# Forget bias of the sample's keys: from two f32r pieces in operands of eight key places to three bf16 pieces in operands of four

## The chip, the core and the metric

The kernel runs on one core of a Trainium2 chip. Five engines work side by side, each through its own list of instructions in order: TensorE (PE in the profile, and PEld for its weight loads), VectorE (DVE), ScalarE (ACT), GpSimd (POOL) and SyncE (SP), which here does little but issue DMAs. The metric is the device time of one execution in microseconds; a kernel's time is the median of its runs.

## The reference

One inference step of a decoder layer for a prompt of 512 tokens and for a sample of 8 sequences with 8 new tokens each, whose past of 2048 keys lies in pages. Two attentions run side by side (forgetting attention, "fox", and a sparse attention, "nsa", of which the sample needs selected blocks, a window and compressed keys), then gates, projections and an MLP. The part that matters here is the forgetting attention of the sample:

```python
cf = jnp.cumsum(lf_all, axis=1)                       # running sum of the log forget values, per head
s = jnp.einsum('btgrd,bsgd->bgrts', q, k) * HEAD_DIM ** -0.5
bias = cq[..., :, None] - ck[..., None, :]            # sum of log forget values between key and query
p = masked_softmax(s + bias, k_pos <= q_pos)
```

Every key of the past gets, for each of 8 heads, the sum of the log forget values of all keys behind it, added to its scores. The sums must be good to about f32.

## The kernel before

The program runs in stages: compression of the sample's cached keys, the input projection, the prompt's attention (`prompt_attention`, at its end the "fox" steps), the sample's attention (`sample_attention`), then the gates and branch projections (`mix_part`, tiles `mg` and `br`), the output projection and the MLP. A scheduler orders the instructions of each engine by simulated times, so an added or shortened instruction can move its neighbours. In the sample's attention the order of PE is the order of the code: `link` ties each matmul behind the one before.

The sample's attention goes over 32 units, unit `u` being a quarter `i = u % 4` of the past of sequence `b = u // 4`, 512 keys each. On PE a round of its loop holds, in this order:

- `key_rows(u + 1)`: eight 128x128 transposes of the next unit's keys (tile `k`, from rows `fr` of the fox cache and `sr` of the nsa cache), copied to SBUF (`kt`) by ACT and by DVE.
- `unit_scores(u)`, L1691: the scores of both attentions in one PSUM bank `ss`. Partitions 0 to 63 hold fox (8 heads x 8 tokens), 64 to 127 nsa. Query times keys is an f32 matmul for each half (`bdF`, `bdN`, two passes each). Then comes the mask of selected blocks, one bf16 matmul of 512 columns into partitions 64 to 127 (L1699, `scr` in the profile), and then the forget bias, four matmuls of 128 columns into partitions 0 to 63 (L1702, `ss<-DT,E`).
- In the third unit of a sequence `new_scores` (tile `sn`) and, with it, `forget_turned(b + 1)` (tile `dt`); in every eighth unit (`u % 8 == 3`) `window_scores` (tile `sw`).
- `values(u - 3)` (tile `so`): weights times values as matmuls of 32 output partitions, and `turn_weights(u - 2)` (tile `sp`): four transposes of softmax weights, copied to `spT` by ACT and DVE in turn.

DVE takes the scores out of `ss` (`sS`, L1707) with the running maximum, ACT does the exponentials.

The forget bias is prepared in four steps. `Dt[p, b, c, h]` holds the log forget value of key place `c` (16 of them) on partition `p`. `forget_sums` (L682, near the end of the prompt's attention) adds up each half of 8 places, sums over the later partitions with one matmul (`xsuf`), and puts into place 0 and place 8 what lies behind their half. `forget_split` (L1674) splits 64 numbers (8 places x 8 heads) into an f32r part by ACT and a remainder by DVE, 2 x 64 rows for each half. `forget_turned` (L1681) turns both halves over with two PE transposes, and DVE copies them to `DT`. In `unit_scores` the constant `E` (zeros and ones from `tok` and `hot`) then adds, for key place `c`, the places behind it in its half and place 0 of the half. `DH` and `DT` have two buffers each, so the split for a sequence waits for the transposes of the second before it.

Loads of `fr` and `sr` are issued by SP about 7 units ahead, as buffers come free; the first units' loads follow right behind the prompt's attention.

Of the kernel before, what the change touches and what calls it, by code (L numbers as in the profile page):

```python
# [6 lines left out]
F32 = mybir.dt.float32  # L7
F32R = mybir.dt.float32r
BF16 = mybir.dt.bfloat16
I32 = mybir.dt.int32  # L10
AF = mybir.ActivationFunctionType
OP = mybir.AluOpType
AX = mybir.AxisListType

P = 128
# [3 lines left out]
NB = 8  # L19
# [26 lines left out]
class Step:  # L46
# [635 lines left out]
    def forget_sums(self, pn):  # L682


        self.scr, self.cut = pn.tile([P, 1024], F32, tag="wide", name="fscr"), 0
        triS = self.carve([P, P])
        self.ts(triS, self.jp, 0.0, None, OP.is_lt)
        half = self.carve([P, 2 * NB, 8])
        with self.tc.issue_after(self.last_min):
            self.nc.vector.tensor_reduce(half, self.Dt.rearrange("p b (a c) h -> p (b a) h c", a=2), axis=AX.X, op=OP.add)  # L690
        hv = half.rearrange("p (b a) h -> p b a h", a=2)
        tot = self.carve([P, NB, 8])
        self.tt(tot, hv[:, :, 0], hv[:, :, 1], OP.add)
        xb = self.accb("xsuf")
        self.mm(xb[:, 0:64], triS, tot.rearrange("p b h -> p (b h)"), True, True)
        xv = xb[:, 0:64].rearrange("p (b h) -> p b h", h=8)
        self.cp(self.Dt[:, :, 8, :], xv)
        self.tt(self.Dt[:, :, 0, :], xv, hv[:, :, 1], OP.add)

    def norm_scaled(self, sq, n, i, x, junk=None):  # L700

# [774 lines left out]
    def sample_tables(self):  # L1476


        nc, slope, gp = self.nc, self.slope, self.nc.gpsimd
        self.scr, self.cut = self.znp.tile([P, 4 * (TOK - C_N)], F32, tag="zN", name="scr"), 0  # L1480
        self.selT = self.carve([P, 256]).bitcast(BF16).rearrange("p (b n) -> p b n", b=NB)
        gp.memset(self.selT, 0.0)
        self.act(self.selT[:32], self.selF.rearrange("p (b n) -> p b n", b=NB))

        self.bhot = self.carve([P, 1024]).bitcast(BF16).rearrange("p (c n) -> p c n", c=16)

        self.nbA, self.nbW = self.carve([P, NB * 72]), self.carve([P, 320])
        self.rw = self.carve([P, SEQ])
        self.ramp = self.carve([P, 2048])
        mark = self.cut  # L1490
        self.cut -= 2048
        ei, hot = self.carve([P, 32]), self.carve([P, 32])
        self.iota(ei, [[1, 32]])
        self.ts(hot, ei, self.prow, None, OP.is_equal)
        self.act(self.bhot.rearrange("p c (a n) -> p (c a) n", a=2), hot[:, :, None].to_broadcast([P, 32, 64]))

        gp.memset(self.nbA, NEG)
        gp.memset(self.nbW, NEG)
        tmask, tramp = self.carve([P, NB, 8]), self.carve([P, NB, 8])
        self.iota(tmask, [[0, 8], [1, 8]])  # L1500
        self.ts(tramp, tmask, slope, None, OP.mult)
        self.ts(tmask, tmask, self.t_row, NEG, OP.is_gt, OP.mult)
        self.tt(tramp, tramp, tmask, OP.add)
        nbf = self.carve([NS, NB, 8])
        self.tt(nbf, self.nbf, tmask[:NS], OP.add)
        own = self.nbA.rearrange("p (b x) -> p b x", x=72)[:, :, 0:8]
        self.cp(own[0:64], nbf)
        self.cp(own[64:128], tramp[64:128])
        own = self.nbW.rearrange("p (i x) -> p i x", x=80)
        for o in range(2):  # L1510
            self.cp(own[64 * o:64 * o + 64, :, 8 * o:8 * o + 8], tramp[64 * o:64 * o + 64, 0:4])
        rw = self.rw
        self.iota(rw, [[1, 4], [4, P]])
        wm = self.carve([P, SEQ])
        self.ts(wm, rw, self.t_row, NEG, OP.is_le, OP.mult)
        self.ts(rw, rw, -512.0, slope, OP.add, OP.mult)
        self.tt(rw, rw, wm, OP.add)
        self.cut = mark


        self.tok, self.hot = self.carve([P, 8]), self.carve([P, 64])
        lim, ej = self.carve([P, 1]), self.carve([P, 8])
        self.iota(ej, [[1, 8]])
        self.ts(lim, self.h_row, 0.0, 8.0, OP.is_equal, OP.mult)
        self.tt(lim, lim, self.h_row, OP.add)
        self.ts(self.tok, ej, lim, None, OP.is_lt)
        self.ts(self.hot.rearrange("p (h t) -> p h t", t=8), ej[:, :, None].to_broadcast([P, 8, 8]), self.t_row, None, OP.is_equal)

        low = self.carve([P, 1])
        self.ts(low, self.prow, 64.0, slope, OP.is_ge, OP.mult)  # L1530
        self.iota(self.ramp, [[1, 2048]], base=-2048)
        gp.tensor_scalar(self.ramp, self.ramp, low, None, op0=OP.mult)
# [27 lines left out]

    def sample_attention(self, sp, sp0):
        nc = self.nc
        self.E = self.op2.tile([P, 8, 64], F32R, name="E")
        self.tt(self.E, self.tok[:, :, None].to_broadcast([P, 8, 64]), self.hot[:, None, :].to_broadcast([P, 8, 64]), OP.mult)
        self.chain = ""
        self.wk, self.S, self.SN, self.SW, self.DT, self.T, self.stat, self.OA = {}, {}, {}, {}, {}, {}, {}, {}
        self.sob, self.acc = self.accb("so"), self.accb("accS")
# [10 lines left out]
        for u in range(4 * NB + 4):  # L1578
            b, i, n, x = u // 4, u % 4, u // 8, u % 8
# [92 lines left out]
        self.keys[u] = out  # L1672

    def forget_split(self, sp, b):  # L1674
        self.DH = DH = self.op2.tile([P, 2, 2, 64], F32R, tag="DH", bufs=2, name=f"DH{b}")
        for hf in range(2):
            d = self.Dt[:, b, 8 * hf:8 * hf + 8, :].rearrange("p c h -> p (c h)")
            self.act(DH[:, hf, 0, :], d)
            self.tt(DH[:, hf, 1, :], d, DH[:, hf, 0, :].bitcast(F32), OP.subtract)

    def forget_turned(self, sp, b):  # L1681
        tb = self.mmb(f"dt{b}")
        for hf in range(2):
            self.tr(tb[:, P * hf:P * hf + P], self.DH[:, hf].rearrange("p a n -> p (a n)").bitcast(F32))
        self.DT[b] = self.op2.tile([P, 2, P], F32R, tag="DT", bufs=2, name=f"DT{b}")
        self.cp(self.DT[b], tb[:, 0:256].rearrange("p (a n) -> p a n", a=2))

    def queries(self, b):
        return [t[:, b].rearrange("p g r t -> p (g r t)") for t in (self.bdF, self.bdN)]
# [1 line left out]
    def unit_scores(self, sp, u):  # L1691

        b, i = u // 4, u % 4
        qF, qN = self.queries(b)
        kf, ks = self.keys.pop(u)
        pb = self.mmb(f"ss{u}")
        self.mm(pb[0:64, :], qF, kf, True, False)
        self.mm(pb[64:128, :], qN, ks, True, False)
        self.mm(pb[64:128, :], self.selT[:, b, :], self.bhot[:, 4 * i:4 * i + 4].rearrange("p c n -> p (c n)"), False, True)  # L1699
        for j in range(4):  # L1700
            c = 4 * i + j
            self.mm(pb[0:64, P * j:P * j + P], self.E[:, c % 8, :], self.DT[b][:, c // 8, :], False, True)  # L1702
        if i == 0:
            self.stat[b] = [self.small.tile(sh, F32, tag=f"ss{x}", name=f"ss{x}_{b}")
                            for x, sh in enumerate(([P, 2, 3], [P, 2, 3], [P, 2]))]
        self.S[u] = sp.tile([P, 512], F32, tag="S", bufs=4, name=f"sS{u}")
        self.nc.vector.tensor_tensor_reduce(self.S[u], pb, self.ramp[:, 512 * i:512 * i + 512], 1.0, LOW, OP.add, OP.max,  # L1707
                                            self.stat[b][0][:, i // 2, i % 2:i % 2 + 1])
# [724 lines left out]
```

## Time and profile before

| what | us |
|---|---|
| runs | 1212.0, 1212.29, 1216.9 |
| median | 1212.29 |
| profiled execution | 1216.62 |
| its span (first to last instruction) | 1214.9 |

The profiled execution is 4.3 us above the median, close to the slowest of the three. Sums are made against the profiled execution, and the difference is then taken from the median.

How the profile is read: a row of the timeline is start, duration, engine, line, operation, output <- inputs, shapes, count. Matmuls are pipelined, so the duration of one includes its way through the array (a 64-column bf16 weight load alone shows 0.11 us); what a matmul costs is the distance from its start to the start of the next. A row with x4 spans from the first start to the last end. All PE matmuls share line L77 and all transposes L83, so one goes by tiles.

| stretch of the span, us | what | PE busy | PE clock granted | DMA share |
|---|---|---|---|---|
| 395 to 437 | prompt's fox attention | 39.09 of 42 | 0.92 | 0.49 |
| 437 to 456 | its end, first keys of the sample | 17.41 of 19 | 1.00 | 0.31 |
| 592 to 700 | gates and branches | 107.21 of 108 | 1.00 | 0.54 |

The sample's attention lies between the last two rows.

### The profile page before, as it was taken

The numbers are of one execution on the slowest core, as the hardware profiler recorded it, in microseconds if no ns is written. First come the engines' busy times: TensorE is split into PE (matmuls) and PEld (weight loads), VectorE is DVE, ScalarE is ACT, GpSimd is POOL, SyncE is SP. The second block draws the span as 40 slices with busy tenths as digits, with TensorE's granted clock in tenths as the row PEclk, the third lists the DMA queues.
The fourth block names the chain that finished last, engine by engine and source line by source line (L and its number), as shares of the span: only waits on it lengthen the run. The fifth ranks groups of instructions, "written<-read, shape, count | busy, mean of one in ns | idle before, by whom it ended". The sixth has DMA issues, their size and how long they took to land.

```text
span 1214.9 us, 24824 instructions
## 1 busy us (share of the span) xinstructions
PE 1168.3 (96%) x9319; PEld 1003.8 (83%) x9319; DVE 768.3 (63%) x1984; ACT 557.8 (46%) x1187; POOL 155.0 (13%) x172
## 2 busy tenths in 40 slices
PE   3899999999999999999999999998999999999998
PEld 3887789899666556666799999998999997888886
DVE  3688785586798856665643335667667853655486
ACT  2455453443776754544532233355565655322230
POOL 1012100000311130000300100001455500000000
PEclk9999999999999999999999999998999999999999
DMA  9599546795776359979863334345344545446302
GB/s 209 161 246 272 167 149 216 239 321 176 240 259 180 90 169 301 316 230 297 204 175 87 87 83 134 108 142 184 129 146 138 173 149 188 150 162 200 109 28 79
DMA packets 168826, 215.37 MB, mean 177 GB/s; under 512 B 18297, under 2 KB 140610, under 8 KB 166530
## 3 DMA queue, kind: packets, MB, share of 16 engines
q1 hardware_dynamic: 147650, 174.21, 46.7%
q0 software_dynamic: 9216, 25.16, 6.7%
q10 hardware_dynamic: 11840, 14.42, 4.0%
q8 instruction: 73, 1.20, 0.4%
q14 instruction: 47, 0.39, 0.1%
HBM read 190.11 MB, written 44.53 MB: 193 GB/s over the span
## 4 chain that ended last, share of the span: by engine, by line
PE 82%; DMA 5%; DVE 5%; SPq 3%; ACT 2%; issue 1%; ACTq 0%; DVEq 0%; POOLq 0%
PE dn L77 16%; PE mg L77 8%; PE z L77 6%; PE hid L77 5%; PE ss L77 4%; PE br L77 4%; PE wo L77 4%; PE k L83 2%; SPq L155 2%; PE up L77 2%; PE so L77 2%; PE ct L83 2%; DMA cpg<-in_cache_nsa_kv 2%; PE sp L83 1%; PE ada L77 1%
## 5 line engine op out<-in xcount | busy, mean ns | idle before, releaser
L77 PE MATMUL z<-winh,h 128*128 128x264 f32 (+1 forms) x576 | 111.0, 286 | 1.1 <-ACT winh L112 0.8
L77 PEld LDWEIGHTS z<-winh,h 128*128 128x128 f32 x576 | 91.7, 190 | 3.2 <-ACT winh L112 1.0
L77 PE MATMUL z<-winl,h 128*128 128x264 f32 (+1 forms) x320 | 88.2, 284 | 0.5 <-DVE winl L131 0.5
L77 PE MATMUL mg<-hH,wml 128*128 128x288 f32 x256 | 75.3, 296 | 0.6 <-DVE wml L131 0.6
L112 ACT ACTIVATE xh<-ct 128x256 fp32r<-128x256 f32 x128 | 48.0, 384 | 59.9 <-PE ct L83 35.2
L77 PE MATMUL mg<-hH,wmh 128*128 128x288 f32 x256 | 75.3, 296 | 0.0
L100 DVE TENSOR_TENSOR acc<-acc,dn 128x512 f32<-128x512 f32 x60 | 41.2, 686 | 51.2 <-PE dn L77 51.1
L77 PE MATMUL mg<-hL,wmh 128*128 128x288 f32 x256 | 72.6, 294 | 0.0
L131 DVE TENSOR_TENSOR xl<-ct,xh 128x256 fp32r<-128x256 f32 x128 | 51.8, 421 | 15.7 <-ACT xh L112 13.9
L77 PEld LDWEIGHTS z<-winl,h 128*128 128x128 f32 x320 | 60.6, 190 | 0.7 <-DVE winl L131 0.7
L83 PE MATMUL ct<-identF,ro 128*128 128x128 f32 x256 | 36.0, 279 | 22.4 <-DVE ro L115 22.1
L131 DVE TENSOR_TENSOR wml<-wmr,wmh 128x1024 fp32r<-128x1024 f32 x14 | 17.2, 1226 | 56.4 <-ACT wmh L112 56.4
L83 PEld LDWEIGHTS ct<-identF,ro 128*128 128x128 f32 x256 | 29.5, 145 | 25.6 <-DVE ro L115 18.8
L77 PEld LDWEIGHTS mg<-hH,wml 128*128 128x128 f32 x256 | 48.1, 188 | 0.8 <-DVE wml L131 0.8
L77 PEld LDWEIGHTS mg<-hH,wmh 128*128 128x128 f32 x256 | 48.1, 188 | 0.2
L77 PEld LDWEIGHTS mg<-hL,wmh 128*128 128x128 f32 x256 | 47.2, 188 | 0.1
L131 DVE TENSOR_TENSOR wp<-sums,wp 128x1024 fp32r<-128x1024 f32 x26 | 39.9, 1541 | 11.0 <-ACT wp L112 10.3
L77 PE MATMUL hid<-xh,w1hlk 128*128 128x512 f32 (+1 forms) x160 | 44.9, 369 | 0.1
L77 PE MATMUL hid<-xh,w1hlv 128*128 128x512 f32 (+1 forms) x160 | 44.0, 361 | 0.8 <-ACT xh L112 0.5
L112 ACT ACTIVATE mgt<-mg 128x288 f32<-128x288 f32 x32 | 12.9, 410 | 59.6 <-PE mg L77 59.6
L1707 DVE CUSTOM_DVE_ANT_0 sS<-ss,scr 128x512 f32<-128x512 f32 x32 | 22.1, 692 | 26.2 <-PE ss L77 26.2
L112 ACT ACTIVATE u<-u 128x1152 f32<-128x1152 f32 x29 | 33.7, 1161 | 10.1 <-DVE u L100 9.4
(1160 smaller groups left out, 3643.4 us busy)
## 6 DMA issues: line engine op xcount, KB each, us to landing
adw<-in_w_ada SPq DMA_DIRECT2D x16, 1024.0 KB
foxD<-in_cache_fox_kv SPq DMA_DIRECT2D x128, 128.0 KB
wdr<-in_w_down SPq DMA_DIRECT2D x32, 512.0 KB
cpg<-in_cache_nsa_kv SPq DMA_DIRECT2D x120, 128.0 KB
fr<-foxD SPq DMA_DIRECT2D x28, 512.0 KB
sr<-in_cache_nsa_kv SPq DMA_DIRECT2D x112, 128.0 KB
pu<-in_w_up SPq DMA_DIRECT2D x26, 512.0 KB
uD<-u ACTq DMA_DIRECT2D x16, 576.0 KB
```

The costliest lines, as they stand in the source:

```text
L77: ins = self.nc.tensor.matmul(out, a, b, start=start, stop=stop, skip_group_check=True)
L83: ins = self.nc.tensor.transpose(out, in_, self.identF[:n, :n])
L100: self.nc.vector.tensor_tensor(out, a, b, op=op)
L112: return self.nc.scalar.activation(out, in_, f, **kw)
L131: self.splits.append((eng or self.nc.vector).tensor_tensor(l, x, h.bitcast(F32), op=OP.subtract).ins)
L155: self.issued[eng] = getattr(self.nc, eng).dma_start(out, in_).ins
L1707: self.nc.vector.tensor_tensor_reduce(self.S[u], pb, self.ramp[:, 512 * i:512 * i + 512], 1.0, LOW, OP.add, OP.max, self.stat[b][0][:, i / ...
```

## The change

The 16 places are cut into four quarters of 4 places instead of two halves of 8, and the numbers into three bf16 pieces that add up to the f32 number, instead of an f32r part and a remainder: 3 pieces x 4 places x 8 heads = 96 rows for an operand. `E` shrinks from 8 to 4 sets of 64 columns and becomes bf16. `forget_sums` writes places 0, 4, 8 and 12.

```diff
@@ forget_sums
-        half = self.carve([P, 2 * NB, 8])
+        part = self.carve([P, 4 * NB, 8])
         with self.tc.issue_after(self.last_min):
-            self.nc.vector.tensor_reduce(half, self.Dt.rearrange("p b (a c) h -> p (b a) h c", a=2), axis=AX.X, op=OP.add)
-        hv = half.rearrange("p (b a) h -> p b a h", a=2)
+            self.nc.vector.tensor_reduce(part, self.Dt.rearrange("p b (a c) h -> p (b a) h c", a=4), axis=AX.X, op=OP.add)
+        pv = part.rearrange("p (b a) h -> p b a h", a=4)
+        self.tt(pv[:, :, 2], pv[:, :, 2], pv[:, :, 3], OP.add)
+        self.tt(pv[:, :, 1], pv[:, :, 1], pv[:, :, 2], OP.add)
         tot = self.carve([P, NB, 8])
-        self.tt(tot, hv[:, :, 0], hv[:, :, 1], OP.add)
+        self.tt(tot, pv[:, :, 0], pv[:, :, 1], OP.add)
...
-        self.cp(self.Dt[:, :, 8, :], xv)
-        self.tt(self.Dt[:, :, 0, :], xv, hv[:, :, 1], OP.add)
+        self.cp(self.Dt[:, :, 12, :], xv)
+        for a in range(3):
+            self.tt(self.Dt[:, :, 4 * a, :], xv, pv[:, :, a + 1], OP.add)
@@ sample_tables
-        self.ts(lim, self.h_row, 0.0, 8.0, OP.is_equal, OP.mult)
-        self.tt(lim, lim, self.h_row, OP.add)
+        self.ts(pos, self.h_row, 4.0, -4.0, OP.is_ge, OP.mult)
+        self.tt(pos, pos, self.h_row, OP.add)
+        self.ts(lim, pos, 0.0, 4.0, OP.is_equal, OP.mult)
+        self.tt(lim, lim, pos, OP.add)
@@ sample_attention
-        self.E = self.op2.tile([P, 8, 64], F32R, name="E")
-        self.tt(self.E, self.tok[:, :, None].to_broadcast([P, 8, 64]), self.hot[:, None, :].to_broadcast([P, 8, 64]), OP.mult)
+        self.E = self.op2.tile([P, 4, 64], BF16, name="E")
+        self.tt(self.E, self.tok[:, 0:4, None].to_broadcast([P, 4, 64]), self.hot[:, None, :].to_broadcast([P, 4, 64]), OP.mult)
@@ forget_split
-        self.DH = DH = self.op2.tile([P, 2, 2, 64], F32R, tag="DH", bufs=2, name=f"DH{b}")
-        for hf in range(2):
-            d = self.Dt[:, b, 8 * hf:8 * hf + 8, :].rearrange("p c h -> p (c h)")
-            self.act(DH[:, hf, 0, :], d)
-            self.tt(DH[:, hf, 1, :], d, DH[:, hf, 0, :].bitcast(F32), OP.subtract)
+        self.DH = DH = self.op2.tile([P, 4, 3, 32], BF16, tag="DH", bufs=2, name=f"DH{b}")
+        rest = self.op2.tile([P, 4, 32], F32, tag="DR", bufs=1, name=f"DR{b}")
+        d = self.Dt[:, b].rearrange("p (a c) h -> p a (c h)", a=4)
+        self.act(DH[:, :, 0], d)
+        self.tt(rest, d, DH[:, :, 0], OP.subtract)
+        self.act(DH[:, :, 1], rest)
+        self.tt(DH[:, :, 2], rest, DH[:, :, 1], OP.subtract)
@@ forget_turned
-        for hf in range(2):
-            self.tr(tb[:, P * hf:P * hf + P], self.DH[:, hf].rearrange("p a n -> p (a n)").bitcast(F32))
-        self.DT[b] = self.op2.tile([P, 2, P], F32R, tag="DT", bufs=2, name=f"DT{b}")
-        self.cp(self.DT[b], tb[:, 0:256].rearrange("p (a n) -> p a n", a=2))
+        for a in range(4):
+            self.mm(tb[:96, P * a:P * a + P], self.DH[:, a].rearrange("p x n -> p (x n)"), self.identB, True, True)
+        self.DT[b] = self.op2.tile([P, 4, P], BF16, tag="DT", bufs=2, name=f"DT{b}")
+        self.cp(self.DT[b][:96], tb[:96].rearrange("p (a n) -> p a n", a=4))
@@ unit_scores
         for j in range(4):
-            c = 4 * i + j
-            self.mm(pb[0:64, P * j:P * j + P], self.E[:, c % 8, :], self.DT[b][:, c // 8, :], False, True)
+            self.mm(pb[0:64, P * j:P * j + P], self.E[:96, j, :], self.DT[b][:96, i, :], False, True)
```

The scheduler's answer moves instructions at three places that matter. The first is PE in a unit's scores, here the third unit of the first sequence, before (`scr` is the mask of selected blocks; an f32 or f32r matmul loads its weights itself and shows no row for it):

```order
L77 MATMUL ss_6703<-kt_2_6654,bdF 64x512
L77 MATMUL ss_6703<-kt_2_6661,bdN 64x512
L77 LDWEIGHTS scr
L77 MATMUL ss_6703<-scr 64x512
L77 MATMUL ss_6703<-DT_6460,E 64x128 x4
L77 MATMUL sn_6713<-knT,bdF 64x64
L77 MATMUL sn_6713<-knT,bdN 64x64
L83 MATMUL dt_6718<-identF,DH_6677 128x128 x2
```

And the same place now, up to the second of the four bias matmuls:

```order
L77 MATMUL ss_6713<-kt_2_6663,bdF 64x512
L77 MATMUL ss_6713<-kt_2_6670,bdN 64x512
L77 LDWEIGHTS scr
L77 MATMUL ss_6713<-scr 64x512
L77 LDWEIGHTS E
L77 MATMUL ss_6713<-DT_6469,E 64x128
```

The order is the same; each of the four bias matmuls now has a weight load of its own in front, and mask and bias are both bf16 and both 64 output partitions wide.

The second place, right behind it on PE, is the turning over of the next sequence's pieces (`dt`), now, from the fourth bias matmul to the first of four turning matmuls:

```order
L77 LDWEIGHTS E
L77 MATMUL ss_6713<-DT_6469,E 64x128
L77 MATMUL sn_6723<-knT,bdF 64x64
L77 MATMUL sn_6723<-knT,bdN 64x64
L77 LDWEIGHTS DH_6686
L77 MATMUL dt_6728<-identB,DH_6686 96x128
```

Two transposes of 128x128 have become four bf16 matmuls with the identity, 96 output partitions each.

The third place is DVE near the end of the prompt's attention, where it works through score tiles (`Sfox`), query tiles (`qstfox`) and tables of the sample side by side. Before:

```order
L109 SCALAR_TENSOR_TENSOR qstfox_5908<-qfox_5903,gcol,qstfox_5908 64x512
L100 TENSOR_TENSOR E<-scr 128x512
L309 TENSOR_REDUCE adw<-adat_6038 128x18
L1228 ISA Sfox_6140,nmfox_6141<-sfox_6144,browfox_5914 128x128
L1228 ISA nmfox_6141 128x1
```

And now:

```order
L109 SCALAR_TENSOR_TENSOR qstfox_5908<-qfox_5903,gcol,qstfox_5908 64x512
L100 TENSOR_TENSOR scr<-scr 128x1
L309 TENSOR_REDUCE adw<-adat_6038 128x18
L1231 ISA Sfox_6142,nmfox_6143<-sfox_6146,browfox_5914 128x128
L1231 ISA nmfox_6143 128x1
```

The making of `E` has left this place; with half the columns it stands 18 rows further down, and a 1-column instruction for `lim` stands here instead. On PE two score tiles of this stretch (256 and 384 columns) now stand ahead of eight `ofox` matmuls instead of behind them. SP's list is unchanged row by row, and POOL's but for one exchange of two rows.

More of the change, by code (lines that the diff above doesn't have):

```diff
@@ L1521, in sample_tables @@
         self.tok, self.hot = self.carve([P, 8]), self.carve([P, 64])
-        lim, ej = self.carve([P, 1]), self.carve([P, 8])
+        lim, pos, ej = self.carve([P, 1]), self.carve([P, 1]), self.carve([P, 8])
         self.iota(ej, [[1, 8]])
-        self.ts(lim, self.h_row, 0.0, 8.0, OP.is_equal, OP.mult)
-        self.tt(lim, lim, self.h_row, OP.add)
+        self.ts(pos, self.h_row, 4.0, -4.0, OP.is_ge, OP.mult)
+        self.tt(pos, pos, self.h_row, OP.add)
+        self.ts(lim, pos, 0.0, 4.0, OP.is_equal, OP.mult)
+        self.tt(lim, lim, pos, OP.add)
         self.ts(self.tok, ej, lim, None, OP.is_lt)
```

## Prediction

> **What bounds the kernel now.** I read the page first: the engines' busy times, then the chain that ended last.
>
> ```profile
> PE 1168.3 (96%) x9319; PEld 1003.8 (83%) x9319; DVE 768.3 (63%) x1984; ACT 557.8 (46%) x1187; POOL 155.0 (13%) x172
> ...
> PE 82%; DMA 5%; DVE 5%; SPq 3%; ACT 2%; issue 1%; ACTq 0%; DVEq 0%; POOLq 0%
> ```
>
> PE is busy 96% of the span and carries 82% of the chain, so time taken from PE's list where PE doesn't wait comes off the end. The windows view says whether it waits in the stage of the change:
>
> ```profile
> 456.00:592.00 136.00, 135.94 (x2010) 90.03 (x2006) 81.28 (x282) 62.83 (x164) 5.17 (x9) 1.00 0.85 273
> ```
>
> PE works 135.94 of 136 us at the full clock, DVE 81 and ACT 63; DMA is at 0.85 of its time. So this stage is PE's, and DMA is the next to look at. The timeline of PE and PEld shows one unit's scores:
>
> ```profile
> 488.06 0.59 PE L77 MATMUL ss<-kt,bdF 128*64 128x512 f32 x1
> 488.07 0.59 PE L77 MATMUL ss<-kt,bdN 128*64 128x512 f32 x1
> 488.07 0.11 PEld L77 LDWEIGHTS <-scr 128*64 128x64 bf16 x1 [0.29 <-issue]
> 488.50 0.38 PE L77 MATMUL ss<-scr 128*64 128x512 bf16 x1
> 488.81 0.31 PEld L77 LDWEIGHTS ss<-DT,E 128*64 128x64 f32 x4 [0.62 <-issue]
> 488.81 0.46 PE L77 MATMUL ss<-DT,E 128*64 128x128 f32 x4
> 489.19 0.25 PE L77 MATMUL so<-fr,spT 128*32 128x64 f32 x2
> ```
>
> Two things are to be seen. The f32 matmuls into the two halves of the partitions start 0.01 us apart: two 64-wide matmuls stream side by side. The mask and the bias also go into different halves, yet the bias starts 0.31 behind the mask, with its first weight load at that moment, and the next group 0.38 behind that: **0.69 us from mask to next group, one behind the other**. What such a distance holds is read from three rows. How long 512 columns take at one piece per number:
>
> ```profile
> 432.77 0.40 PE L77 MATMUL sfox<-klfox,qstfox 128*128 128x512 f32 x1
> 433.00 0.23 PE L77 MATMUL sfox<-diagB,identB 128*128 128x128 bf16 x1
> ```
>
> 0.23 us, so the mask's 0.31 holds some 0.08 in which nothing streams. How far apart the four bias matmuls are:
>
> ```profile
> L77 PE MATMUL ss<-DT,E x128: 220/223/275, 456.9 to 590.5; 128*64 128x128 f32 x128
> ```
>
> The four cover 0.46 and the last lasts 0.22, so it starts 0.24 behind the first; the first lasts 0.275, 0.055 longer than the others, which is its own weight load. That leaves 0.06 from one to the next: later weight loads hide behind the matmul before. And what follows:
>
> ```profile
> 456.56 0.38 PE L77 MATMUL ss<-scr 128*64 128x512 bf16 x1
> 456.87 0.46 PE L77 MATMUL ss<-DT,E 128*64 128x128 f32 x4
> 457.16 0.40 PE L83 MATMUL k<-identF,fr 128*128 128x128 f32 x2
> ...
> 462.50 0.38 PE L77 MATMUL ss<-scr 128*64 128x512 bf16 x1
> 462.81 0.45 PE L77 MATMUL ss<-DT,E 128*64 128x128 f32 x4
> 463.19 0.27 PE L77 MATMUL sn<-knT,bdF 128*64 128x64 f32 x1
> ```
>
> A full-width transpose (`k`) follows the last bias matmul (457.11) by 0.05, its own streaming; a 64-wide one (`sn`) or a 32-wide one (`so`) by 0.14, so 0.09 more. Mask (64 wide) to bias also pays 0.08. The f32r bias behaves like a full-width matmul: a change of width costs 0.08 to 0.09 before and behind it, and it can't stand beside the mask. The Trainium skill's page TensorEngine Tiling (Key Properties) says that a change of tiling mode drains TensorE and that tiles of one mode work independently. The trace agrees, with 0.09 beside 0.05 here and 0.01 for the pair; by that rule the bf16 bias, as wide as the mask, overlaps it.
>
> **The change, part by part.** *Mask and bias.* In bf16 the bias is a second 64-wide matmul behind the mask, in the other half. I take it to start with the mask, its first weight load not hidden: 0.055, three distances of 0.06, 0.055 of streaming, 0.29 in all, longer than the mask's 0.23. Then 0.09 for the change of width before `so` (18 units) and before `k` (units 0 and 1), and none before `sn` (8 units) and `sw` (4 units), which are 64 wide. So 0.38 instead of 0.69 in 18 units (5.6 us), 0.29 instead of 0.69 in 12 (4.8), 0.38 instead of 0.60 in 2 (0.4): **-10.8 us**. Bounds: with the first load hidden as the mask's is, 0.055 x 32 = 1.8 more; with no overlap, the second rival.
>
> *Turning.* The distance of f32 transposes of 128 columns, and `dt` before:
>
> ```profile
> 486.62 0.60 PE L83 MATMUL k<-identF,fr 128*128 128x128 f32 x4
> 487.05 0.60 PE L83 MATMUL k<-identF,sr 128*128 128x128 f32 x4
> ```
> ```profile
> 532.75 0.44 PE L83 MATMUL dt<-identF,DH 128*128 128x128 f32 x2
> 533.11 0.25 PE L77 MATMUL so<-fr,spT 128*32 128x64 f32 x2
> ```
>
> Four transposes in 0.43, 0.11 each, so the two of `dt` cost 0.22 of their 0.36; the rest is the change of width, which stays. A bf16 matmul with 96 weight columns is in no row; between the bias's 0.06 (64 columns) and 0.11 (128) I take 0.08, nearest by columns: 4 x 0.08 - 0.22 = 0.1, in 8 sequences **+0.8 us** (0.2 to 1.8).
>
> *ACT and DVE behind it.* Per sequence DVE now copies 96x512 instead of 128x256, and the split is a chain ACT, DVE, ACT, DVE of 128 numbers each, where two independent pairs of 64 stood:
>
> ```profile
> L115 DVE CAST DT<-dt x8: 419/420/424, 453.7 to 568.8; 128x256 fp32r<-128x256 f32 x8
> ```
> ```profile
> L115 DVE COPY kt<-k 128x512 f32<-128x512 f32 x31 | 21.4, 691 | 10.1 <-PE k L83 10.0
> ```
> ```profile
> L112 ACT ACTIVATE DH<-Dt x16: 238/240/258, 437.3 to 533.4; 128x64 fp32r<-128x64 f32 x16
> L100 DVE TENSOR_TENSOR DH<-Dt,DH x16: 213/217/220, 438.3 to 533.8; 128x64 fp32r<-128x64 f32 x16
> ```
> ```profile
> 534.63 0.69 DVE L115 COPY spT<-sp 128x512 f32<-128x512 f32 x1
> ```
> ```profile
> 538.57 0.25 PE L77 MATMUL so<-fr,spT 128*32 128x64 f32 x2
> ```
>
> The copy grows by 0.27 (a 512-column copy takes 0.69) and the chain by some 0.5, one more ACT and one more DVE instruction that wait for each other. Behind the waiting piece on ACT stands the next unit's `kt`, which waits for PE's transposes anyway; behind that on DVE stands `spT`, done at 535.32, and `so` asks for it behind the next unit's scores, at 538.57, 3.2 us later. So a delay of 0.8 stays hidden; without that cover it would be 0.8 in 7 sequences, 5.6 us. I take 0.
>
> *Loads.* Keys must be there when a faster PE asks.
>
> ```profile
> PEld k L83 <- DMA sr<-in_cache_nsa_kv: 0.5, 2, 0.3
> ```
> ```profile
> 460.88 0.14 PEld L83 LDWEIGHTS k<-identF,sr 128*128 128x128 f32 x1 [0.20 <-DMA sr<-in_cache_nsa_kv]
> ```
> ```profile
> 522.60 1.92 SPq L155 DMA_DIRECT2D sr<-in_cache_nsa_kv  x4
> ```
> ```profile
> 534.43 0.60 PE L83 MATMUL k<-identF,fr 128*128 128x128 f32 x4
> ```
>
> The waits view has one place where PE waits for keys, unit 3's, up to 460.88. The 0.44 that units 0 and 1 save is lost in that wait, and perhaps part of unit 2's: **+0.6**. Later the loads run ahead: unit 20's last issue ends at 524.5 and its transposes start at 534.4, 10 us later.
>
> *Prompt's end.* The reduce in `forget_sums` reads as many numbers; four DVE instructions of 64 numbers, about the 0.22 of the `DH` row each, come in. `E`'s making has half the columns and leaves its place:
>
> ```profile
> 418.22 0.69 DVE L100 TENSOR_TENSOR E<-scr 128x512 fp32r<-128x512 f32 x1
> ```
> ```profile
> 419.11 0.51 PE L77 MATMUL sfox<-khfox,qstfox 128*128 128x384 f32 x1 [1.07 <-DVE adw L309]
> ```
> ```profile
> 420.00:422.00 2.00, 2.00 (x9) 1.34 (x8) 1.88 (x11) 1.20 (x3) 0.61 (x1) 0.50 0.00 0
> ```
> ```profile
> 424.00:426.00 2.00, 2.00 (x8) 0.67 (x6) 0.25 (x3) 1.15 (x5) 0.00 (x0) 0.50 1.00 126
> ```
>
> PE's wait of 1.07 for the reduction right behind `E` should halve, but DVE meets the added work before the next wait for it: I take 0. The granted clock is 0.50 from the first to the last of these three windows, 420 to 426, with PE busy for 5.5 us; if the shorter wait keeps the clock up, up to half of that goes, 2.7 us. The other bound is +1, the added DVE instructions.
>
> *Sum.* -10.8 + 0.8 + 0.6 = **-9.4 us**. The profiled execution of 1216.62 would come to 1207.2; the median of 1212.29, 4.3 below it, to **1203**. A measurement tells 0.5%, 6.06 us, from no change, so faster means under 1206.2.
>
> **The rivals.** *No overlap.* The bias doesn't get beside the mask, but its loads stay hidden: it starts at 0.23, its last ends at 0.465, so 0.555 before `so` and `k`, 0.465 before `sn` and `sw`: 18 x 0.135 + 12 x 0.225 + 2 x 0.045 = 5.2, less 0.8 and 0.1, so -4.3: 1208. For it speaks that no row shows a bf16 matmul beside another; against it the f32 pair.
>
> *Slower: weight loads wait for the matmul in flight.* Each of the four then costs its load and its streaming, 0.055 + 0.06 = 0.115, behind the mask: 0.23 + 0.46 = 0.69, 0.78 with the change of width. That is 18 x 0.09 + 0 + 2 x 0.18 = +2.0; turning costs 4 x (0.08 + 0.055) - 0.22 = 0.32 in 8 sequences, +2.6. Together +4.6: 1217. It decides as soon as mask and bias together take more than 0.69. Against it: the mask's load starts at 488.07 while `bdN` streams through the same rows and columns, and the bias loads hide today. The Trainium skill's page TensorE: Matmul & The Clock Gate (What overlaps and what doesn't) says that a weight load overlaps matmuls in flight only where the row groups differ. Here they don't differ, so by that rule this rival holds; the trace speaks against the rule.
>
> *Loads bind.* If keys come when they come now until unit 11, what the first 11 units save is lost: 0.44 + 4 x 0.40 + 5 x 0.31 = 3.6 instead of 0.6, so -6.4: 1206. For it: DMA at 0.85 of the whole stage. Against it: one wait of 0.5 us.
>
> *The clock stays up* in the prompt's end: 2.7 more, 1200.
>
> **How the numbers follow.** Forecast 0.55, no overlap 0.18, slower 0.10, loads 0.10, clock 0.07. Faster by over 0.5%: nearly all of the forecast and the clock, half of the loads, a little of the second: 0.68. Slower by over 0.5% (above 1218.4) is the upper part of the slower rival: 0.04. Within: 0.28. The range goes from 1198.5 (clock, or the first load hidden too) to 1210 (no overlap, 0.8 to 1.8 for turning); outside are the slower rival and tails.
>
> **What would show it.** In the timeline the first `ss<-DT,E` starts within 0.06 of `ss<-scr` (overlap) or 0.2 or more behind it (no overlap), and the group behind starts 0.3 to 0.4 after the mask. Four `dt` take 0.3. PE stays at its full share from 456 on, with few waits for `sr`; the stage up to the first `mg` is about 9 us shorter. It would be wrong if the distance to the next group stays near 0.69, or if PE gets waits for `kt`, `spT` or `sr` in most units.

## The result, and the profile after

| | before | changed |
|---|---|---|
| runs, us | 1212.0 to 1216.9 (6) | 1200.37 to 1205.93 (6) |
| median | 1214.72 | 1203.89 |
| profiled execution | 1216.62 | 1203.84 |
| its span | 1214.9 | 1202.0 |

Changed against before: ratio 0.9912, 95% interval 0.9898 to 0.9927. By the medians that is 10.8 us less, by the two spans 12.9.

The page of the changed kernel, its engines, beside the row at the start of the prediction:

```profile
PE 1156.1 (96%) x9335; PEld 1003.1 (83%) x9335; DVE 770.0 (64%) x1990; ACT 559.0 (47%) x1187; POOL 154.7 (13%) x172
```

PE is busy 12.2 us less and carries 83% of the chain that ended last (82% before); the other engines moved by under 2 us. So the time came off PE's list. The timeline of PE and PEld in the changed kernel, the first unit's scores and the first copy behind them:

```profile
456.38 0.59 PE L77 MATMUL ss<-kt,bdF 128*64 128x512 f32 x1
456.38 0.11 PEld L77 LDWEIGHTS <-E 96*64 96x64 bf16 x1 [0.29 <-issue]
...
456.39 0.11 PEld L77 LDWEIGHTS <-scr 128*64 128x64 bf16 x1
456.81 0.22 PE L77 MATMUL ss<-DT,E 96*64 96x128 bf16 x1
456.81 0.22 PEld L77 LDWEIGHTS <-E 96*64 96x64 bf16 x3 [0.31 <-issue]
456.82 0.38 PE L77 MATMUL ss<-scr 128*64 128x512 bf16 x1
...
457.13 0.31 PEld L83 LDWEIGHTS k<-identF,fr 128*128 128x128 f32 x3
```

The first bias matmul (`ss<-DT,E`) starts with the mask (`ss<-scr`), 0.01 ahead of it, although it stands behind it in the program. Its weight load starts 0.43 earlier, while query times keys streams. From mask to `k` it is 0.31 (before 0.60). The same block in front of `so`, and in front of `sn` and `dt`:

```profile
474.01 0.22 PE L77 MATMUL ss<-DT,E 96*64 96x128 bf16 x1
474.01 0.38 PE L77 MATMUL ss<-scr 128*64 128x512 bf16 x1
```
```profile
474.32 0.25 PE L77 MATMUL so<-fr,spT 128*32 128x64 f32 x2
```

```profile
462.90 0.38 PE L77 MATMUL ss<-scr 128*64 128x512 bf16 x1
462.96 0.33 PE L77 MATMUL ss<-DT,E 96*64 96x128 bf16 x3
463.12 0.22 PE L77 MATMUL sn<-knT,bdN 128*64 128x64 f32 x1
...
463.33 0.42 PE L77 MATMUL dt<-identB,DH 128*96 128x128 bf16 x4
463.60 0.61 PE L83 MATMUL sp<-identF,sS 128*128 128x128 f32 x4
```

Mask to `so` is 0.31 (before 0.69), mask to `sn` 0.22 (before 0.69), and the four `dt` take 0.27 up to `sp`. The windows of the stage in the changed kernel:

```profile
456.00:580.00 124.00, 122.49 (x2024) 87.25 (x2024) 83.04 (x285) 63.95 (x165) 5.18 (x9) 1.00 0.92 298
```

PE now idles 1.5 us of 124 where it idled 0.06 of 136, and DMA is at 0.92 instead of 0.85. The waits view of PE in this window names two waits, and in the timeline a weight load of PE waits a third time, for the keys of unit 10 (tile `rows`):

```profile
PE k L83 <- DMA sr<-in_cache_nsa_kv: 0.7, 1, 0.7
PE so L77 <- ACT spT L112: 0.6, 3, 0.2
```
```profile
488.70 0.14 PEld L83 LDWEIGHTS k<-identF,rows 128*128 128x128 f32 x1 [0.34 <-DMA rows<-in_cache_nsa_kv]
```

**Where the time went.** The stage runs from the first `ss` to the first `mg`, first before and then now:

```profile
455.64 0.64 PE L77 MATMUL ss<-kt,bdF 128*64 128x512 f32 x1
```
```profile
591.61 0.38 PE L77 MATMUL mg<-hH,wmh 128*128 128x288 f32 x1
```
```profile
455.90 0.64 PE L77 MATMUL ss<-kt,bdF 128*64 128x512 f32 x1
```
```profile
579.99 0.38 PE L77 MATMUL mg<-hH,wmh 128*128 128x288 f32 x1
```

That is 135.97 us before and 124.09 now, -11.9 of the spans' -12.9; the start moved by +0.3, and the part behind the first `mg` is 1.3 shorter (623.3 and 622.0). In the ten kernels of this study that last part takes between 619.3 and 624.2 us without regard to what was changed, and the first `ss` starts between 453.6 and 456.2. Together, what lies outside the stage takes between 1073.6 and 1079.9 us, so a single span carries some 6 us that follow no edit, and the experiments below are read by this stage and by ratios of runs.

From one unit's first `ss` to the next unit's, the two timelines show the same saving again and again: 0.38 us in a unit with `so` behind its scores, 0.53 to 0.55 where `sn` or `sw` stands there, 0.26 in unit 0. The exceptions are units 12, 20 and 28 (0.10 saved instead of 0.38), 4 (0.25), 8 (0.06) and 1 (0.41 lost); they hold the waits above, and unit 4 a shorter one for `spT` (0.07).

### The profile page after: what moved, and what is told of

Read it like the earlier page. It is cut to its first block, busy times and chain, and to the rows that moved or that the text cites. A ratio compares the mean times of both kernels' runs of the same rounds, so it can differ in the third digit from the quotient of the medians.

```text
span 1202.0 us, 24863 instructions
## 1 busy us (share of the span) xinstructions
PE 1156.1 (96%) x9335; PEld 1003.1 (83%) x9335; DVE 770.0 (64%) x1990; ACT 559.0 (47%) x1187; POOL 154.7 (13%) x172
## 4 chain that ended last, share of the span: by engine, by line
PE 83%; DMA 5%; DVE 5%; SPq 3%; ACT 3%; issue 2%; ACTq 0%; DVEq 0%; POOLq 0%
PE dn L77 16%; PE z L77 9%; PE mg L77 8%; PE hid L77 6%; PE br L77 4%; PE wo L77 4%; PE ss L77 2%; SPq L155 2%; PE up L77 2%; PE ct L83 2%; PE k L83 2%; DMA cpg<-in_cache_nsa_kv 2%; PE ada L77 2%; PE so L77 2%; PE sp L83 1%
## 5 line engine op out<-in xcount | busy, mean ns | idle before, releaser
L112 ACT ACTIVATE mgt<-mg 128x288 f32<-128x288 f32 x32 | 12.9, 410 | 58.5 <-PE mg L77 58.5
L131 DVE TENSOR_TENSOR wp<-pu,wp 128x512 fp32r<-128x512 f32 (+1 forms) x26 | 27.2, 1050 | 16.9 <-ACT wp L112 16.9
```

What stands on the lines that cost most here:

```text
L112: return self.nc.scalar.activation(out, in_, f, **kw)
L131: self.splits.append((eng or self.nc.vector).tensor_tensor(l, x, h.bitcast(F32), op=OP.subtract).ins)
```

## Experiments

Each table figure is from one profiled execution, from the first start of `ss<-kt,bdF` to the first of `mg<-hH,wmh`; the ratio is that of the runs against before.

| kernel | stage, us | ratio | interval |
|---|---|---|---|
| before | 136.0 | 1 | |
| changed | 124.1 | 0.9912 | 0.9898 to 0.9927 |
| f32r_bias | 135.4 | 1.0008 | 0.9992 to 1.0024 |
| wide_bf16 | 136.3 | 1.0001 | 0.9985 to 1.0018 |
| nomask_after | 123.1 | 0.9906 | 0.9880 to 0.9932 |
| nomask_before | 130.0 | 0.9959 | 0.9942 to 0.9976 |
| f32_narrow | 142.4 | 1.0045 | 1.0027 to 1.0062 |
| mask_first | 123.8 | 0.9919 | 0.9903 to 0.9934 |
| dh3 | 123.4 | 0.9910 | 0.9890 to 0.9930 |
| kt_first | 123.4 | 0.9914 | 0.9897 to 0.9932 |

### Only the type undone: f32r_bias

```diff
-        self.E = self.op2.tile([P, 4, 64], BF16, name="E")
+        self.E = self.op2.tile([P, 4, 64], F32R, name="E")
...
-        self.DT[b] = self.op2.tile([P, 4, P], BF16, tag="DT", bufs=2, name=f"DT{b}")
+        self.DT[b] = self.op2.tile([P, 4, P], F32R, tag="DT", bufs=2, name=f"DT{b}")
```

> The changed kernel with one thing undone: E and DT are f32r again instead of bf16. The 96 rows, the four quarters, the preparation, the turning and the order of the prompt's end stay as in the changed kernel. Theory (the gain is mask and bias side by side, and an f32r matmul runs at full width whatever its operand's columns): the first bias matmul starts 0.31 us behind the mask instead of with it, and the next group 0.69 behind the mask instead of 0.22 to 0.31. Per round 0.38 in 18 units, 0.47 in 12 and 0.29 in 2 come back, 13.1 us, less the 1 us that the wait for unit 3's keys takes up: +12 us against the changed kernel, ratio to before 1.000 (0.998 to 1.002). Rival (the gain comes from the preparation, the smaller copies of E or the moved rows in the prompt's end): the time stays within 3 us of the changed kernel, ratio 0.990 to 0.993.

Ratio 1.0008: the whole gain is gone. The timeline of this kernel:

```profile
472.65 0.38 PE L77 MATMUL ss<-scr 128*64 128x512 bf16 x1
472.96 0.45 PE L77 MATMUL ss<-DT,E 96*64 96x128 f32 x4
473.34 0.11 PEld L77 LDWEIGHTS so<-fr,spT 128*32 128x32 f32 x2
```

Mask to bias 0.31, mask to `so` 0.69, the numbers of before, although the preparation, the smaller copies, 96 rows and the four quarters are all in. From unit to unit it takes what the kernel before takes, to 0.02 us; only unit 1 is 0.48 shorter, by its wait for keys. So none of those parts gains or costs anything that can be measured; the gain hangs on the type of the four matmuls.

### Type kept, width undone: wide_bf16

```diff
-        self.E = self.op2.tile([P, 4, 64], BF16, name="E")
+        self.E = self.op2.tile([P, 4, 128], BF16, name="E")
+        nc.vector.memset(self.E, 0.0)
...
-            self.mm(pb[0:64, P * j:P * j + P], self.E[:96, j, :], self.DT[b][:96, i, :], False, True)
+            self.mm(pb[:, P * j:P * j + P], self.E[:96, j, :], self.DT[b][:96, i, :], False, True)
```

> The changed kernel with the bias kept in bf16, but E padded with 64 columns of zeros, so that each bias matmul goes to all 128 output partitions and adds zero to the lower half (same result). Theory (what counts is the width, not the type): a full-width matmul can't stand beside the 64-wide mask, so it starts 0.31 behind it; the next group comes 0.60 to 0.69 behind the mask instead of 0.22 to 0.31, about 0.35 more in 18 units, 0.45 in 12, 0.27 in 2: +12 us, less 1 in the wait for unit 3's keys, so +11 against the changed kernel, ratio to before 0.998 to 1.001. Rival (the type counts: a bf16 bias is cheaper in itself, for example through weight loads of its own that hide): the next group stays within 0.45 of the mask and the kernel within 5 us of the changed one, ratio below 0.995.

Ratio 1.0001, as the theory of the width has it. A bf16 bias of 128 columns stands behind the mask like the f32r one:

```profile
475.68 0.38 PE L77 MATMUL ss<-scr 128*64 128x512 bf16 x1
475.99 0.40 PE L77 MATMUL ss<-DT,E 96*128 96x128 bf16 x4
476.32 0.11 PEld L77 LDWEIGHTS so<-fr,spT 128*32 128x32 f32 x2
```

0.31 to the bias and 0.64 to `so`. The type alone is worth the last 0.05 (0.64 against 0.69; the four take 0.40 instead of 0.45). Over 32 units that would be 1.8 us, and the stage doesn't show it, because in this execution PE waits 1.1 and 0.9 us for unit 3's keys. The two runs together say that the gain needs a matmul that really runs 64 wide; f32r with a 64-column operand behaves like the wide one.

### Without the mask: nomask_after and nomask_before

In both kernels the one line of the mask's matmul is left out.

```diff
-        self.mm(pb[64:128, :], self.selT[:, b, :], self.bhot[:, 4 * i:4 * i + 4].rearrange("p c n -> p (c n)"), False, True)
```

> The changed kernel without the mask-of-selected-blocks matmul (it leaves the mask out of the nsa scores; 32 matmuls of 512 columns less, all else as it was). Theory (mask and bias stream side by side, and the bias is the longer or as long): the group behind comes at the same distance, 0.22 to 0.31 behind the first bias matmul; 0 to -1 us against the changed kernel. Rival (the two don't overlap and the gain came from elsewhere): the mask's own streaming goes, 0.23 x 32 = 7.4, so -7 us, ratio to before about 0.985.

> The kernel before without the mask-of-selected-blocks matmul (it leaves the mask out of the nsa scores). Theory (before, mask and bias stood one behind the other): the mask's streaming of 0.23 goes in 32 units, 7.4 us, while the change of width in front of the f32r bias stays, since query times keys is 64 wide too: -7 us against before, ratio 0.994; at most the whole 0.31 in each, -10 us, ratio 0.992. Rival (the mask cost nothing before either): 0 to -1 us, ratio 0.999 to 1.000.

Changed kernel: stage 124.1 to 123.1, and the intervals of the ratios (0.9906 and 0.9912) lie over each other; bias to `so` stays at 0.31:

```profile
471.77 0.39 PE L77 MATMUL ss<-DT,E 96*64 96x128 bf16 x4
472.08 0.25 PE L77 MATMUL so<-fr,spT 128*32 128x64 f32 x2
```

From unit to unit this kernel and the changed one agree to 0.005 us, but for units 1 and 8: there the changed kernel loses 0.7 and 0.3 to waits for keys that this execution doesn't have. So the 1.0 isn't the mask's; beside the bf16 bias it costs nothing that shows.

Kernel before: ratio 0.9959, 5.0 us by the ratio and 5.95 by the stage. So the mask cost 5 to 6 us when it stood in front of the f32r bias. Expected were 7; the distance from second query pass to bias fell from 0.75 to 0.53, 0.22 x 32 = 7.0. Of the missing 1.1, PE's wait for unit 3's keys holds 0.3, waits for ACT's `spT` in units 12, 20 and 28 hold 0.3, and a gap of PE ahead of two `sp` transposes at 550.10 holds 0.4; what PE waited for there, the view doesn't say. The mask's 0.31 was thus not all its own: the 0.09 of the change of width stays in front of the bias without it.

### The same width in another type: f32_narrow

```diff
-        self.E = self.op2.tile([P, 8, 64], F32R, name="E")
+        self.E = self.op2.tile([P, 8, 64], F32, name="E")
...
-        self.DT[b] = self.op2.tile([P, 2, P], F32R, tag="DT", bufs=2, name=f"DT{b}")
+        self.DT[b] = self.op2.tile([P, 2, P], F32, tag="DT", bufs=2, name=f"DT{b}")
```

> The kernel before with E and DT as plain f32 instead of f32r, so that each bias matmul takes two passes, like query times keys, which runs 64 wide and side by side. Theory (the type counts only through the width that it runs at): the first bias matmul starts within 0.06 of the mask, though the two have different types; at the 0.43 to 0.47 us that a pass of 512 columns takes in query times keys, the four last 0.86 to 0.95, with 0.09 more in front of a 32-wide or full-width group. To the next group 0.95 to 1.04 in 18 units, 0.86 to 0.95 in 12, 0.95 to 1.04 in 2, instead of 0.69, 0.69 and 0.60: +9 us against before (+6 to +11), ratio 1.005 to 1.009. Rival (only matmuls of one type stand side by side): the bias starts 0.3 behind the mask and the rest comes on top: +19 us, ratio 1.015.

Slower, 1.0045, and its timeline shows why it is still on the theory's side:

```profile
463.19 0.27 PE L77 MATMUL ss<-DT,E 128*64 128x128 f32 x1
463.20 0.38 PE L77 MATMUL ss<-scr 128*64 128x512 bf16 x1
463.30 0.82 PE L77 MATMUL ss<-DT,E 128*64 128x128 f32 x6
463.85 0.27 PE L77 MATMUL sn<-knT,bdN 128*64 128x64 f32 x1
463.96 0.27 PE L77 MATMUL ss<-DT,E 128*64 128x128 f32 x1
463.96 0.22 PE L77 MATMUL sn<-knT,bdN 128*64 128x64 f32 x1
464.06 0.28 PE L77 MATMUL sn<-knT,bdF 128*64 128x64 f32 x2
```

An f32 bias starts with a bf16 mask, so equal types aren't needed; eight passes of 0.11 then last longer than the mask hides. The loss is 5.5 us by the ratio, 6.5 by the stage, where +9 was expected; the ratio lies a little below its range of 1.005 to 1.009. Units with `so` behind lose 0.26 to 0.27, the low end of what was expected. The 12 units with `sn` or `sw` behind lose 0.11 to 0.12 where at least 0.17 was expected: the nsa half goes on with `sn` while the fox half still has bias to do, which the sum had not allowed for. And PE waits 0.5 less for unit 3's keys.

### The order of the mask: mask_first

```diff
+        self.mm(pb[64:128, :], self.selT[:, b, :], self.bhot[:, 4 * i:4 * i + 4].rearrange("p c n -> p (c n)"), True, False)
         self.mm(pb[0:64, :], qF, kf, True, False)
-        self.mm(pb[64:128, :], qN, ks, True, False)
-        self.mm(pb[64:128, :], self.selT[:, b, :], self.bhot[:, 4 * i:4 * i + 4].rearrange("p c n -> p (c n)"), False, True)
+        self.mm(pb[64:128, :], qN, ks, False, True)
```

> The changed kernel with the mask ahead of query times keys instead of behind it (same sum). In the nsa half of the partitions now stand mask and two passes of query times keys, in the fox half two passes and the bias. Theory (each half works through its own list, whatever stands between in program order): the fox half starts with the mask, the bias starts as soon as the fox passes are through, and both halves take about as long as before: 0 against the changed kernel, -1 to +1 us, ratio to before 0.990 to 0.992. Rival (the halves work in step and only neighbours overlap): mask 0.23, then the passes, then the bias 0.25 alone: 0.2 in 32 units, +6 to +7 us, ratio to before about 0.996.

```profile
474.81 0.40 PE L77 MATMUL ss<-scr 128*64 128x512 bf16 x1
474.82 0.64 PE L77 MATMUL ss<-kt,bdF 128*64 128x512 f32 x1
475.05 0.59 PE L77 MATMUL ss<-kt,bdN 128*64 128x512 f32 x1
475.30 0.59 PE L77 MATMUL ss<-kt,bdF 128*64 128x512 f32 x1
475.48 0.59 PE L77 MATMUL ss<-kt,bdN 128*64 128x512 f32 x1
475.73 0.39 PE L77 MATMUL ss<-DT,E 96*64 96x128 bf16 x4
```

The nsa half runs 0.23, then 0.18 behind the fox half through the passes, and the bias fills the end of the fox half beside the last nsa pass. Ratio 0.9919, stage 123.8: no difference from the changed kernel, as the theory said. What counts is the sum in each half, not the neighbours in the program.

### The waits at the start of the stage: dh3 and kt_first

The timelines of the changed kernel ahead of the first `ss`, ACT and PE:

```profile
453.96 0.31 ACT L112 ACTIVATE DH<-Dt 128x128 bf16<-128x128 f32 x1 [3.72 <-PE dt L77]
```
```profile
454.81 1.16 PE L83 MATMUL k<-identF,rows 128*128 128x128 f32 x8 [0.89 <-ACT kt L112]
```

PE waits 0.89 for ACT's `kt` (454.18, right behind the `DH` row), and ACT stood 3.7 us in front of it, at a piece of a later sequence (`DH`) that waits for `dt`. Two kernels tried to take that away: a third buffer for `DH`, and one exchange on ACT that puts `kt` in front of that piece.

```diff
@@ dh3
-        self.DH = DH = self.op2.tile([P, 4, 3, 32], BF16, tag="DH", bufs=2, name=f"DH{b}")
+        self.DH = DH = self.op2.tile([P, 4, 3, 32], BF16, tag="DH", bufs=3, name=f"DH{b}")
@@ kt_first
-            (self.cp if n else self.act)(k, tb)
+            ins = (self.cp if n else self.act)(k, tb)
+            if u + n == 0:
+                self.first_kt = ins.ins
...
-        self.act(DH[:, :, 0], d)
+        with self.tc.issue_after(self.first_kt) if b > 1 else nullcontext():
+            self.act(DH[:, :, 0], d)
```

> The changed kernel with three buffers for DH instead of two: ACT's first piece for the third sequence no longer waits for the turning of the first, and the first kt behind it on ACT comes 0.9 us earlier. Theory (the wait for unit 3's keys in the sr load stands behind it and takes up what is gained ahead of it): 0 against the changed kernel, the wait of PE for kt at the start goes and the wait for sr grows by as much; ratio to before 0.990 to 0.992. Rival (the loads start earlier too, since buffers come free earlier): -1 us, ratio 0.9905 or less.

> The changed kernel with one exchange on ACT: the first copy of keys (kt of unit 0) stands ahead of the third sequence's first piece (DH), which waits for the turning of the first sequence. In the changed kernel kt stood behind it, and PE waited 0.89 for kt at 454.8. Theory (the load of unit 3's sr keys is issued when DVE has written oT, whatever PE does, and PE waits for it at 461): PE's wait for kt goes, the first ss starts 0.9 earlier against oT, and the wait for unit 3's sr grows from 0.7 to 1.6; 0 against the changed kernel, ratio to before 0.990 to 0.992. Rival (the keys' loads come earlier with PE, or the wait for sr was due to something else): the wait stays at 0.7 and 0.9 us are gained, ratio about 0.9905; a time alone can't tell these apart, the two waits in the trace can.

Neither moved the time (0.9910 and 0.9914), but neither did what it was built to do, so my theory about unit 3's keys was not tested by them. In dh3 the scheduler used the third buffer to issue one more sequence's pieces early, and the fourth sequence's piece took the third's place in front of `kt`; PE still waits 0.89. In kt_first `kt` comes early, and PE waits one step further on, in the waits view:

```profile
PE k L83 <- PE k L83: 1.0, 1, 1.0
```

that is at the second half of unit 1's transposes (453.05). They start when DVE has copied unit 0's second `kt`; that they wait for the PSUM bank of that copy is read from the times, the view doesn't name it. DVE gets to the copy behind `oT` (450.92) and the copy of `dt`:

```profile
451.66 0.69 DVE L115 CAST DT<-dt 96x512 bf16<-96x512 f32 x1
452.26 0.68 DVE L115 COPY kt<-k 128x512 f32<-128x512 f32 x1
```

So the wait of 0.9 seems to have two ends that fall close together, ACT's `kt` and DVE's, and taking away one shows the other. In kt_first PE then has no wait for unit 3's keys at all, and in dh3 one of 0.1, with the first `ss` as far behind `oT` as in the changed kernel (2.7 us): the changed kernel's 0.7 differs from execution to execution, and what sets it stays open.

## Why the prediction was right, and where its terms were off

**Mask and bias** (forecast -10.8): right in its mechanism, and shown by f32r_bias, wide_bf16 and nomask_after. Its size was taken too small. I charged the first weight load of the bias with 0.055, and the rows show it hidden behind query times keys like the mask's (456.38, with the mask's at 456.39). A block is then 0.22 instead of 0.29, and 0.31 with the change of width instead of 0.38. From the rows: 18 x 0.38 + 12 x 0.47 + 2 x 0.29 = 13.1 us, about the bound that the prediction gave for this case (12.6). What the prediction put at nothing is a gain in the 12 units behind the scores themselves. The first `sn` of a half took 0.05 longer than the second before, and takes as long now:

```profile
L77 PE MATMUL sn<-knT,bdF x16: 222/246/270, 463.2 to 586.4; 128*64 128x64 f32 x16
```
```profile
L77 PE MATMUL sn<-knT,bdF x16: 220/221/222, 463.1 to 575.1; 128*64 128x64 f32 x16
```

From `sn` to `dt` it is 0.21 instead of 0.27, and the four `sw` take 1.07 instead of 1.12 up to `so`: 12 x 0.05 = 0.6 us more.

**Turning** (forecast +0.8): -0.1. Four bf16 matmuls of 96 columns take 0.27 up to `sp`, where two f32 transposes took 0.28 before:

```profile
463.45 0.44 PE L83 MATMUL dt<-identF,DH 128*128 128x128 f32 x2
463.73 0.49 PE L83 MATMUL sp<-identF,sS 128*128 128x128 f32 x3
```

In the six other turnings of the stage, with `so` behind, it is 0.35 instead of 0.37. The estimate of 0.08 each, by columns between two rows, was too dear.

**ACT and DVE** (forecast 0): the chain of pieces itself costs nothing, as f32r_bias (1.0008, with the whole chain in) shows. But PE's wait of 0.6 for `spT` is new, and ACT ends it. Three rounds show it, 503.57 the first; its rows on PE, after and before, and ACT's copy, after and before:

```profile
503.57 0.25 PE L77 MATMUL so<-fr,spT 128*32 128x64 f32 x2 [0.21 <-ACT spT L112]
```
```profile
507.40 0.25 PE L77 MATMUL so<-fr,spT 128*32 128x64 f32 x2
```
```profile
502.94 0.57 ACT L112 ACTIVATE spT<-sp 128x512 f32<-128x512 f32 x1
```
```profile
506.66 0.57 ACT L112 ACTIVATE spT<-sp 128x512 f32<-128x512 f32 x1
```

Before, the copy was done at 507.23 and `so` asked at 507.40, 0.17 us of slack behind a row of softmax on ACT. A scores block shorter by 0.38 makes PE ask 0.21 too early. From start to start it costs more than the idle time: `so` stands 0.59 behind the mask in these three units instead of 0.31, and in unit 4, with a wait of 0.07, 0.45. So 3 x 0.28 + 0.14 = 1.0 us is lost. It is PE's speed that brings these waits and not the new preparation: f32r_bias, which has the preparation, lacks them, and nomask_before, which has only the shorter block, has 0.04 in units 12, 20 and 28. The prediction looked at a DVE copy with 3.2 us of slack; this ACT copy had far less, and there three units keep only 0.10 of their 0.38.

**Loads** (forecast +0.6): 1.0. From the first `ss` to the first transpose of the window's keys (`wk`) behind unit 3's it takes 5.4 us before (455.64 to 461.05) and 5.6 now (455.90 to 461.46), though two score blocks in it are 0.29 shorter each: -0.6 is turned into +0.15, a loss of 0.7. Nothing of what units 0 and 1 save arrives. In other executions with the same order on PE this stretch is 5.0 (dh3) and 4.9 (kt_first), so the size of that wait is also a matter of when one load lands. The other 0.3 is the wait for unit 10's keys at 488.70: unit 8's round takes 3.59, where other rounds of its kind take 3.27. The prediction judged the later loads by unit 20's, asked for 10 us after their last issue; unit 10's were asked for 6.7 us after theirs (issued up to 481.68). Kt_first loses 0.3 to the keys of unit 11 instead, dh3 to neither.

**The stage's sum** with these sizes: -13.1 - 0.6 - 0.1 + 1.0 + 1.0 = -11.8, and the stage shows -11.9.

**Prompt's end** (forecast 0): the wait for the reduction did halve, 1.07 to 0.53, but PE waits 0.61 for DVE's `nmfox` at 421.70, where it didn't before, the clock still falls, and no gain shows. The wait and the windows view of the changed kernel, where the prediction showed those of before:

```profile
418.56 0.44 PE L77 MATMUL sfox<-khfox,qstfox 128*128 128x384 f32 x1 [0.53 <-DVE adw L309]
```
```profile
420.00:422.00 2.00, 1.39 (x6) 1.15 (x7) 1.88 (x11) 1.52 (x5) 0.61 (x1) 0.50 0.13 37
```

The granted clock is 0.50 in this window and in the two behind it, up to 426, as before, so the rival in which it stays up didn't come.

**The rivals.** No overlap: refuted by the start of the bias with the mask. Weight loads that wait for the matmul in flight: refuted, since `E`'s load runs while `bdF` streams through the same rows and columns, and three more run beside the mask (456.81, 0.22 for three). The Trainium skill's page TensorE: Matmul & The Clock Gate (What overlaps and what doesn't) says that a weight load overlaps only with other row groups; the trace disagrees. Loads bind: only in two places, units 3 and 10, 1.0 us in all, with DMA at 0.92.

**The size as a whole.** The forecast of 9.3 less by the median stands against 10.8 by the medians and 8.9 to 12.4 by the interval of the ratio. Against the stage, the gain in the scores and right behind them was taken 2.9 too small and `dt` 0.9 too dear, and 1.4 of waits (1.0 for `spT`, 0.4 more for loads) weren't foreseen. The errors go against each other, and that -9.4 lies as near as it does is in part luck. So is the forecast median of 1203 beside 1203.89: the median before came out 2.4 higher than the one that it was taken from.

## What to carry to other kernels

A distance of PE starts that is longer than the streaming of what starts there is worth taking apart: here 0.69 held 0.23 of mask, 0.29 of bias and twice a change of width of 0.08 to 0.09, and a bias that runs 64 wide like the mask put them side by side. Before shortening a matmul, ask which width it really runs at; an operand of 64 columns in f32r gained nothing. Then look for the copy with the least slack on each engine that feeds the next group: the cut it can't follow is lost.

## What the runs showed of the hardware that was not expected

The two 64-wide halves of the array don't keep the program's order between them. In the changed kernel the bias starts 0.01 ahead of the mask. In f32_narrow both passes of `sn`'s `bdN` (463.85 and 463.96) start ahead of the two `bdF` passes (464.06), which stand in front of them in the program, and in mask_first the halves stay 0.18 to 0.23 apart through their passes. The lead is not unlimited: in f32_narrow `bdN` starts 0.65 behind the mask, whose streaming is 0.23, when six of the bias's passes behind the first were on their way. What sets that limit wasn't tried. The Trainium skill's page TensorE: Matmul & The Clock Gate (What overlaps and what doesn't) says that matmuls start and end in program order; between halves the starts in these rows show otherwise (the ends are modelled and can't tell).
